# One decoder layer on one core: the last down group taken out of the block scheme, its free slots used for the mask tables, and three smaller moves

## The chip, the core and the metric

The kernel runs on one core of a Trainium2 chip. The metric is the device time of one execution in microseconds (us), lower is better. The engines that matter are TensorE (PE in the profile: matmuls, with PEld its weight loads), VectorE (DVE), ScalarE (ACT), GpSimd (POOL) and SyncE (SP, which here only issues loads and stores). Each engine runs its own list of instructions in the order in which the program wrote them. It stops at an instruction whose operand is not ready, and then everything behind that instruction on the same engine stops too.

## The reference, cut to what matters

256 tokens of width 2048 go through one layer: a gated feed-forward block (5632 hidden columns), a token mixer with three kinds of attention, and a second feed-forward block.

```python
def _swiglu(h, w_gu, w_down):
    gate, up = jnp.split(h @ w_gu, 2, axis=-1)
    return (jax.nn.silu(gate) * up) @ w_down

def reference(x, ...):
    x = x + 0.5 * _swiglu(_rmsnorm(x, ffn1_norm), ffn1_w_gu, ffn1_w_down)
    x = x + _token_mixing(_rmsnorm(x, mix_norm), ...)
    x = x + 0.5 * _swiglu(_rmsnorm(x, ffn2_norm), ffn2_w_gu, ffn2_w_down)
    return x
...
# mixer C, per head: three softmaxes, over 16 compressed blocks, over selected blocks, over a window
    o = gate[..., 0:1] * o_cmp + gate[..., 1:2] * o_slc + gate[..., 2:3] * o_win
...
    merged = (gates[:, :, 0] * (o_a @ w_branch_a) + gates[:, :, 1] * (o_b @ w_branch_b)
              + gates[:, :, 2] * (o_c @ w_branch_c))
    return merged @ w_out
```

## The kernel before

**Three products for one.** Every large matrix product is made of three passes in a rounded 32-bit format: an operand is split into a rounded part `hi` (ACT copies it) and the rest `lo` (DVE subtracts), and `products` (lines 158 to 160) does hi by hi, lo by hi and hi by lo. The activations are split once, when they are made. The weights are split as they arrive: `emit_split` (lines 116 and 117) makes one ACT copy and one DVE subtraction for each weight tile of 128 x 1024.

**Steps.** All weight work is a list of steps, `subs`. A step is one split weight tile and the matmuls that use it. A plain step has twelve matmuls of 512 columns (two row tiles of weights, two halves of the tokens, three products). There are six raw tiles for arriving weights and four pairs of split tiles; the split of a step is written some three steps ahead of its matmuls (`stream`). Side work, such as transposes, evacuations or attention, is written as Python generators, `chains`. A chain is spawned into a phase of the step ("pre": before the step's last split is written, "mid": after it, "pe": after its matmuls) with a gap in steps. So a gap decides where in each engine's list the next piece of side work stands. Nothing is reordered later.

**Feed-forward.** The 11 blocks of 512 hidden columns are worked in four groups, (0,3), (3,6), (6,9), (9,11). In a group, each block's gate and up products are made, `to_mid` transposes and splits the result into the tile `mid`, and then the group's part of the down product is added to `x_sb`. All products but the first block's are made in pairs of 512 output columns by `add_pair`: part of the contraction goes through a scheme of seven block products in place of eight, a step of six matmuls each. The scheme costs DVE more: sums of weight blocks (line 356, and two accumulating DMAs issued by POOL at lines 402 and 406), differences between PSUM banks (lines 395 and 398), and sums of the activations. Those are made by `sums`, from x by `combos_x` and, once a group, from the middle by `combos_m` (pieces at lines 288 to 292 and 204/205, `ffn_samX`, `ffn_samS`). Each pair takes up to six PSUM banks; `more_banks` and `fewer_banks` move two of the eight banks between the pair scheme (`mains`) and the side work (`banks`).

**Handing over.** `down_evac` (line 479) adds a finished bank pair to `x_sb`. After the last group it spawns `x_prep` of the next stage, which transposes x (line 234) and splits it into `xT` (lines 207 and 208).

**Tables.** The mixers need mask and distance tables. `build` starts at step 52 (`TABLES_AT`), and `build_tables` (lines 534 to 574) makes them in pieces four steps apart, with the `ffn_f` tiles of the first feed-forward block as scratch.

**Mixer C.** `unit_c` works one head on one block of 128 queries, 24 units in all. `apply_p` transposes the probabilities in blocks of 128 keys (line 914), ACT copies them from PSUM (line 921), and `pv` multiplies them with the values (line 1055). The compressed keys are one more block, of 32 rows: it has its own transposes, its own DVE copy (line 923) and its own product over 32 rows (line 1052).

**Merge.** `branch_evac` multiplies each branch's product with its gate (DVE) and adds it up on POOL (line 1154). After the third branch, `to_mT` transposes the sum (line 1133), spawned with a gap of one step.

Of the kernel before, what the change touches and what calls it, by code (L numbers as in the profile page):

```python
# [24 lines left out]
TABLES_AT = 52  # L25
# [22 lines left out]
def hybrid_trunk_kernel(ctx, tc, x, ffn1_norm, ffn1_w_gu, ffn1_w_down, mix_norm, w_in, qk_gain, sinks, cmp_pos,  # L48
# [202 lines left out]
    def add_ffn(norm, w_gu, w_down, done):  # L251
# [46 lines left out]

        def combos_x():
# [10 lines left out]
            yield from sums(*tmp, st["sax"])  # L310
# [133 lines left out]
        def to_mid(kt0):  # L444
# [19 lines left out]
            if kt0 == 0:  # L464
                spawn(combos_m(), "mid", 3)

        def up_evac(kt0, gap):
            def f(bank):
# [3 lines left out]
                spawn(to_mid(kt0), "pe", gap)  # L472
# [13 lines left out]
        for gi, (a, b) in enumerate(groups):  # L486
            for c in range(a, b):
                kt0 = 4 * (c - a)
                up = up_evac(kt0, 1 if c == 10 else 3)
# [8 lines left out]
        li, raw, n, width, mm, before, after, post = subs[-1]  # L498

        def end():  # L500
            after()
            fewer_banks()
        subs[-1] = (li, raw, n, width, mm, before, end, post)


    tabs, scratch = {}, []
# [23 lines left out]
    def build_tables():  # L530
# [12 lines left out]
        yield "mid", 4  # L543
        DVE.scalar_tensor_tensor(m1, D, 127.5, m0, op0=OP.is_le, op1=OP.mult)
        table(tabs["B"], D, m1, m2)
        yield "mid", 4
        DVE.scalar_tensor_tensor(m1, D, 128.5, m0, op0=OP.is_le, op1=OP.mult)
        table(tabs["A"][:, 0], D, m1, m2)
        for g, dil in ((1, 4), (2, 16)):
            yield "mid", 4  # L550
# [6 lines left out]
        yield "mid", 4  # L557
# [34 lines left out]
    def add_mix(done):  # L592
# [6 lines left out]
        def open_mix():  # L599
# [7 lines left out]
            st["vcmp"] = p.tile([32, 64], F32, name="vcmp")  # L607
# [21 lines left out]
            POOL.memset(st["Xs"].bitcast(F32)[:, :, 64:66], 0.0)  # L629

# [205 lines left out]
        def cmp_tail(i, bank):  # L836
# [25 lines left out]
            if i == 1:  # L862
                DVE.tensor_copy(st["vcmp"], b[:32, :64])
# [41 lines left out]
        def apply_p(sb, blocks, pv):  # L905
# [7 lines left out]
            for i, (c0, n) in enumerate(blocks):  # L913
                PE.transpose(place[i][:n], sb[:, c0:c0 + n], ident)
# [3 lines left out]
            full = sum(n == 128 for _, n in blocks)  # L918
            for src, i0, n in ((b, 0, min(full, 4)), (O[:, 256:], 4, full - 4)):
# [18 lines left out]
        def unit_a(h, qb):  # L938
# [21 lines left out]
            blocks = [(g * nk + 128 * kb, 128) for g in range(3) for kb in range(qb + 1)]  # L960
# [16 lines left out]
        def unit_b(pr, qb):  # L977
# [25 lines left out]
            blocks = [(i * nk + 128 * kb, 128) for i in range(2) for kb in range(qb + 1)]  # L1003
# [15 lines left out]
        def unit_c(h, qb):  # L1019
# [27 lines left out]
            blocks = [(32 + 128 * i, 128) for i in range(2 * qb + 2)] + [(0, 32)]  # L1047

            def pv(pt, i):
                c0, n = blocks[i]  # L1050
                if n == 32:
                    PE.matmul(O[:, 0:64], pt[:32, i], st["vcmp"], start=True, stop=True)
                    return
# [89 lines left out]
        def branch_evac(b, oc):  # L1143
            def f(bank):
# [11 lines left out]
                if b == 2:  # L1156
                    spawn(to_mT(mg, oc), "pe", 1)
# [118 lines left out]
    if "mix" in stages:  # L1276
        def build():
# [4 lines left out]
            yield "mid", 1  # L1282
# [29 lines left out]
```

## Time and profile before

| what | value |
|---|---|
| time, median of 3 runs | 2180.73 us (2180.51 to 2181.09) |
| time of the profiled execution | 2181.03 us |
| its span, first to last instruction | 2179.3 us |
| PE busy | 2144.9 us, 98% of the span |
| DVE busy | 1615.8 us, 74% |
| ACT busy | 1247.9 us, 57% |
| POOL busy | 145.5 us, 7% |
| matmul instructions | 10081 |

A row of a timeline has a start, a busy time, the engine, the line, the operation and its tiles, and in brackets the idle time ahead of it with what ended it. Matmuls overlap: a 512-column matmul is shown as 0.39 us long, but the next one starts 0.23 us after it. So PE's pace is read from start to start, not from the busy time.

### The profile page before, as it was taken

Reading aid. Unit: us, or ns where it says so; the run is one execution under the profiler, and the core shown is the slowest. Engines: PE = TensorE matmul, PEld = TensorE weight load, DVE = VectorE, ACT = ScalarE, POOL = GpSimd, SP = SyncE. Lnnn points to the kernel's source line nnn. Section 1 sums busy time; section 2 is a strip of 40 time slices with the busy share of each in tenths; the row PEclk is TensorE's granted clock in tenths of the full one; section 3 lists DMA queues with packets and bytes.
Section 4 is the critical chain, followed back from the end, with each engine's and each line's share of the span. In section 5 each row is a group of like instructions: output and inputs, shape, how many; then the busy total and the mean of one; then the engine's idle time right before and its main releaser. Section 6 shows DMA issues by size and latency. Waiting matters only on the chain. (4 is left out here: it accounts for less than half of the span.)

```text
span 2179.3 us, 27509 instructions
## 1 busy us (share of the span) xinstructions
PE 2144.9 (98%) x10081; PEld 1796.9 (82%) x10081; DVE 1615.8 (74%) x2050; ACT 1247.9 (57%) x1664; POOL 145.5 (7%) x155
## 2 busy tenths in 40 slices
PE   8999999999999999999999999999999999999998
PEld 6887888888887999998888788888888888888886
DVE  7988887888887676666555554557978887887886
ACT  6655665565565566555555444445655665665564
POOL 0000000000000121000000110100000000000000
PEclk9999999999999999999999999999999999999999
DMA  8887878888886574444456666567878878887974
GB/s 287 245 243 222 268 234 230 275 231 244 232 264 171 165 230 134 120 112 141 126 152 191 180 184 193 174 194 240 248 225 269 262 203 268 236 266 205 289 217 142
DMA packets 237600, 463.66 MB, mean 213 GB/s; under 512 B 13384, under 2 KB 42648, under 8 KB 234904
## 3 DMA queue, kind: packets, MB, share of 16 engines
q1 hardware_dynamic: 217368, 403.17, 56.0%
q0 software_dynamic: 20096, 58.72, 15.4%
q8 instruction: 79, 1.29, 0.2%
q14 instruction: 57, 0.47, 0.1%
HBM read 430.39 MB, written 2.10 MB: 198 GB/s over the span
## 5 line engine op out<-in xcount | busy, mean ns | idle before, releaser
L117 DVE TENSOR_TENSOR lo<-raw,hi 128x1024 fp32r<-128x1024 f32 (+3 forms) x561 | 663.9, 1186 | 310.6 <-ACT hi L116 299.1
L116 ACT ACTIVATE hi<-raw 128x1024 fp32r<-128x1024 f32 (+3 forms) x561 | 570.5, 1020 | 322.8 <-PE main L160 255.7
L116 ACT ACTIVATE hi<-ffn_sb 128x1024 fp32r<-128x1024 f32 x392 | 412.5, 1059 | 294.5 <-PE main L160 122.6
L158 PE MATMUL main<-hi,xT 128*128 128x512 f32 (+2 forms) x1480 | 567.7, 384 | 2.9 <-ACT hi L116 2.9
L117 DVE TENSOR_TENSOR lo<-ffn_sb,hi 128x1024 fp32r<-128x1024 f32 x392 | 473.1, 1222 | 125.6 <-ACT hi L116 121.3
L159 PE MATMUL main<-lo,xT 128*128 128x512 f32 (+2 forms) x1480 | 557.9, 377 | 3.2 <-DVE lo L117 3.2
L160 PE MATMUL main<-hi,xT 128*128 128x512 f32 (+2 forms) x1480 | 557.6, 377 | 0.0
L158 PEld LDWEIGHTS main<-hi,xT 128*128 128x128 f32 x1480 | 279.1, 189 | 55.0 <-issue 6.6
L159 PEld LDWEIGHTS main<-lo,xT 128*128 128x128 f32 x1480 | 278.7, 188 | 48.2 <-DVE lo L117 6.5
L160 PEld LDWEIGHTS main<-hi,xT 128*128 128x128 f32 x1480 | 278.3, 188 | 43.5
L159 PE MATMUL main<-lo,ffn_midt 128*128 128x512 f32 x348 | 136.0, 391 | 2.9 <-DVE lo L117 2.9
L158 PE MATMUL main<-hi,ffn_midt 128*128 128x512 f32 x348 | 136.3, 392 | 1.6 <-DVE main L398 1.4
L160 PE MATMUL main<-hi,ffn_midt 128*128 128x512 f32 x348 | 135.6, 390 | 0.0
L356 DVE TENSOR_TENSOR ffn_sb<-ffn_sb,ffn_sb 128x2048 f32<-128x2048 f32 (+1 forms) x72 | 130.9, 1818 | 2.5
L159 PE MATMUL misc<-lo,xT 128*128 128x512 f32 x296 | 115.5, 390 | 1.1 <-DVE lo L117 1.1
L160 PE MATMUL misc<-hi,xT 128*128 128x512 f32 x296 | 115.3, 389 | 0.0
L158 PE MATMUL misc<-hi,xT 128*128 128x512 f32 x296 | 115.3, 389 | 0.0
L159 PEld LDWEIGHTS main<-lo,ffn_midt 128*128 128x128 f32 x348 | 65.4, 188 | 17.7 <-DVE lo L117 4.5
L158 PEld LDWEIGHTS main<-hi,ffn_midt 128*128 128x128 f32 x348 | 65.4, 188 | 15.8 <-DVE main L398 1.8
L158 PE MATMUL misc<-hi,ffn_midt 128*128 128x512 f32 x196 | 76.7, 391 | 1.1 <-DVE misc L398 1.1
L160 PEld LDWEIGHTS main<-hi,ffn_midt 128*128 128x128 f32 x348 | 65.4, 188 | 13.5
L159 PE MATMUL misc<-lo,ffn_midt 128*128 128x512 f32 x196 | 76.4, 390 | 0.0
(276 smaller groups left out, 2742.0 us busy)
## 6 DMA issues: line engine op xcount, KB each, us to landing
raw<-in_ffn_w_gu_dram SPq DMA_DIRECT2D x192, 512.0 KB, 7.3
ffn_sb<-in_ffn_w_gu_dram SPq DMA_DIRECT2D x80, 1024.0 KB, 6.9
raw<-in_ffn_w_down_dram SPq DMA_DIRECT2D x112, 512.0 KB, 5.6
raw<-in_w_in_dram SPq DMA_DIRECT2D x96, 512.0 KB, 3.6
raw<-in_w_in_dram SPq DMA_DIRECT2D x88, 384.0 KB, 3.3
ffn_sb<-in_ffn_w_down_dram SPq DMA_DIRECT2D x64, 512.0 KB, 6.4
ffn_sb<-in_ffn_w_gu_dram POOLq DMA_DIRECT2D x20, 1024.0 KB, 9.8
ffn_sb<-ffn_sb POOLq DMA_DIRECT2D x20, 1024.0 KB, 8.1
```

Of the source, the lines that this page charges most:

```text
L116: ACT.activation(hi, raw, AF.Copy)
L117: DVE.tensor_tensor(lo, raw, hi.bitcast(F32), op=OP.subtract)
L158: PE.matmul(o, lhs(0), hi, start=start, stop=False, **kw)
L159: PE.matmul(o, lhs(0), lo, start=False, stop=False, **kw)
L160: PE.matmul(o, lhs(1), hi, start=False, stop=stop, **kw)
L356: DVE.tensor_tensor(block_buf(i, dst), block_buf(i, a), block_buf(i, b), op=OP.add)
```

## The change

Five edits, all in the order or the form of work:

1. **Last group plain.** For the group (9,11) the four output blocks of the down product are made by `add_chunk`, twelve matmuls a step, and no sums of the middle are made for it. The two banks go back to the side work ahead of that group (`late`), where `fewer_banks` stood at the stage's end.
2. **Tables.** `build` starts at step 90, and `build_tables` waits for `ready_late`, which the last group's first step sets. Its pieces are two steps apart where they were four.
3. **Sums of the middle** in eight pieces, four steps apart, where there were four pieces three steps apart.
4. **Merge transposes** spawned with a gap of two steps.
5. **Compressed values** padded with zero rows from 32 to 128, so that the compressed block is treated as the others are.

```diff
-TABLES_AT = 52
+TABLES_AT = 90
...
-        def sums(a11, a12, a21, a22, dst, gap=1):
-
-            DVE.tensor_tensor(a22, a21, a22, op=OP.subtract)
-            DVE.tensor_tensor(a21, a11, a21, op=OP.subtract)
-            yield "mid", gap
-            DVE.tensor_tensor(a11, a22, a11, op=OP.subtract)
-            DVE.tensor_tensor(a12, a12, a11, op=OP.add)
-            yield "mid", gap
+        def sums(a11, a12, a21, a22, dst, one, two):
+
+            for i, (d, a, b, op) in enumerate(((a22, a21, a22, OP.subtract), (a21, a11, a21, OP.subtract),
+                                               (a11, a22, a11, OP.subtract), (a12, a12, a11, OP.add))):
+                DVE.tensor_tensor(d, a, b, op=op)
+                if (two, one)[i % 2]:
+                    yield "mid", (two, one)[i % 2]
             for i, (n, t) in enumerate((("X5", a22), ("S2", a11), ("X3", a12), ("S3", a21))):
                 split_to(dst[n][:, :, 0], dst[n][:, :, 1], t)
-                if i == 1:
-                    yield "mid", gap
+                if (two, one)[i % 2] and i < 3:
+                    yield "mid", (two, one)[i % 2]
...
-            yield from sums(f[0][:, :, :128], f[1][:, :, :128], f[0][:, :, 128:], f[1][:, :, 128:], st["sam"], 3)
+            yield from sums(f[0][:, :, :128], f[1][:, :, :128], f[0][:, :, 128:], f[1][:, :, 128:], st["sam"], 4, 4)
...
+        def late():
+            fewer_banks()
+            ready_late.append(norm)
...
-            if kt0 == 0:
-                spawn(combos_m(), "mid", 3)
+            if blocks:
+                spawn(combos_m(), "mid", 2)
...
-            for j in (0, 2):
-                add_pair(w_down, 512 * a, 4 * (b - a), NSM, 512 * (j + 1), 512 * j, part_of("mid", st), "sam",
-                         down_evac(j + 1, gi == 3), down_evac(j, gi == 3))
+            for j in range(4):
+                evac = down_evac(j, gi == 3)
+                if b - a == 2:
+                    add_chunk(w_down, 512 * a, 4 * (b - a), 512 * j, 512, part_of("mid", st), evac,
+                              before=late if j == 0 else None)
+                elif j % 2:
+                    add_pair(w_down, 512 * a, 4 * (b - a), NSM, 512 * j, 512 * (j - 1), part_of("mid", st), "sam",
+                             evac, down_evac(j - 1, False))
...
-            st["vcmp"] = p.tile([32, 64], F32, name="vcmp")
+            st["vcmp"] = p.tile([128, 64], F32, name="vcmp")
...
+            POOL.memset(st["vcmp"], 0.0)
...
-            for i, (c0, n) in enumerate(blocks):
-                PE.transpose(place[i][:n], sb[:, c0:c0 + n], ident)
+            for i, c0 in enumerate(blocks):
+                PE.transpose(place[i], sb[:, c0:c0 + 128], ident)
...
-            if full < nb:
-                DVE.tensor_copy(pt[:32, full], place[full][:32])
...
-                    PE.matmul(O[:, 0:64], pt[:32, i], st["vcmp"], start=True, stop=True)
+                    PE.matmul(O[:, 0:64], pt[:, i], st["vcmp"], start=True, stop=True)
...
-                    spawn(to_mT(mg, oc), "pe", 1)
+                    spawn(to_mT(mg, oc), "pe", 2)
...
-            yield "mid", 1
+            while not ready_late:
+                yield "mid", 1
             yield from build_tables()
```

Two places show what moves. The first is DVE's list in the first group of the first feed-forward block, at the pair of the group's third hidden block; `raw` and `ffn_sb` are weight tiles, `lo` is what the split leaves. Before:

```order
L117 TENSOR_TENSOR lo_86<-ffn_sb_158,hi_82 128x1024
L356 TENSOR_TENSOR ffn_sb_158<-ffn_sb_158,ffn_sb_160 128x2048
L205 TENSOR_TENSOR ffn_samX_154<-ffn_f_165,ffn_samX_154 128x2x128
L205 TENSOR_TENSOR ffn_samS_155<-ffn_f_164,ffn_samS_155 128x2x128
L117 TENSOR_TENSOR lo_83<-raw_77,hi_79 128x1024
L117 TENSOR_TENSOR lo_84<-ffn_sb_158,hi_80 128x1024
```

After:

```order
L117 TENSOR_TENSOR lo_86<-ffn_sb_158,hi_82 128x1024
L355 TENSOR_TENSOR ffn_sb_158<-ffn_sb_158,ffn_sb_160 128x2048
L117 TENSOR_TENSOR lo_83<-raw_77,hi_79 128x1024
L290 TENSOR_TENSOR ffn_f_164<-ffn_f_165,ffn_f_164 128x2x128
L117 TENSOR_TENSOR lo_84<-ffn_sb_158,hi_80 128x1024
```

The two pieces between the 2048-wide block sum and the split of `raw_77` are gone from there; one shorter piece stands behind that split.

The second is DVE's list in the last down group of the first feed-forward block, where x gets its sums (line 479 before, 482 after) and `xT` is made (line 208). Before, in the pair scheme:

```order
L117 TENSOR_TENSOR lo_83<-ffn_sb_158,hi_79 128x1024
L356 TENSOR_TENSOR ffn_sb_158<-ffn_sb_158,ffn_sb_160 128x1024
L117 TENSOR_TENSOR lo_84<-raw_75,hi_80 128x1024
L117 TENSOR_TENSOR lo_85<-ffn_sb_158,hi_81 128x1024
L479 SCALAR_TENSOR_TENSOR x_sb<-main_64,x_sb 128x512
L479 SCALAR_TENSOR_TENSOR x_sb<-misc_70,x_sb 128x512
```

After, plain, with a piece of the tables (lines 553 to 557 and 540 to 542 there, 551 to 555 and 538 to 540 before):

```order
L117 TENSOR_TENSOR lo_83<-raw_77,hi_79 128x1024
L482 SCALAR_TENSOR_TENSOR x_sb<-main_65,x_sb 128x512
L482 SCALAR_TENSOR_TENSOR x_sb<-main_66,x_sb 128x512
L117 TENSOR_TENSOR lo_84<-raw_78,hi_80 128x1024
L553 TENSOR_SCALAR ffn_f_165<-ffn_f_164 128x256
L554 CAST ffn_f_165<-ffn_f_165 128x256
L555 CAST ffn_f_165<-ffn_f_165 128x256
L556 SCALAR_TENSOR_TENSOR ffn_f_165<-ffn_f_165,ffn_f_164 128x256
L557 TENSOR_TENSOR ffn_f_165<-ffn_f_165,ffn_f_164 128x256
L540 SCALAR_TENSOR_TENSOR tabA<-ffn_f_164,ffn_f_165 128x256
L541 TENSOR_SCALAR ffn_f_165<-ffn_f_165 128x256
L542 TENSOR_TENSOR tabA<-tabA,ffn_f_165 128x256
```

The block sums of line 356 are gone from the group, the sums into x stand behind a plain split, and eight table operations stand between two splits.

## Rows read from the trace of the kernel before

**Rows 1.** The page: busy times with instruction counts, PE's granted clock by slices.

```profile
PE 2144.9 (98%) x10081; PEld 1796.9 (82%) x10081; DVE 1615.8 (74%) x2050; ACT 1247.9 (57%) x1664; POOL 145.5 (7%) x155
...
PEclk9999999999999999999999999999999999999999
```

**Rows 2.** Waits of PE: line and releaser, us in total, times, longest.

```profile
PE main L159 <- DVE lo L117: 6.2, 10, 0.8
PE main L158 <- DVE x_sb L479: 5.7, 2, 2.9
PE misc L1133 <- POOL mg L1154: 4.5, 4, 1.1
...
PE main L158 <- DVE main L398: 1.4, 1, 1.4
...
PE misc L158 <- DVE misc L398: 1.1, 1, 1.1
...
PE main L158 <- DVE misc L395: 0.6, 1, 0.6
```

**Rows 3.** Stretches: length, PE, PEld, DVE, ACT, POOL busy (count), clock, DMA, GB/s.

```profile
664.10:724.90 60.80, 55.04 (x243) 43.56 (x242) 46.11 (x57) 35.09 (x54) 3.13 (x4) 0.97 0.61 160
2119.98:2175.39 55.41, 50.24 (x219) 39.63 (x217) 40.27 (x44) 26.11 (x31) 3.00 (x3) 1.00 0.54 147
...
695.30:698.00 2.70, 2.70 (x8) 2.09 (x9) 1.57 (x2) 0.06 (x1) 0.83 (x1) 0.56 0.93 245
...
2155.00:2175.00 20.00, 20.00 (x90) 16.54 (x89) 12.79 (x15) 7.43 (x7) 0.00 (x0) 1.00 0.23 69
```

**Rows 4.** Timeline, last down group of the first feed-forward block, PE.

```profile
695.29 0.48 PE L158 MATMUL main<-hi,ffn_samX 128*128 128x512 f32 x1 [2.84 <-DVE x_sb L479]
```

**Rows 5.** The handover to the mixer, DVE's groups of 695 to 733 us.

```profile
L208 DVE SCALAR_TENSOR_TENSOR xT<-misc,cols,xT 128x256 fp32r<-128x256 f32 x16 | 7.4, 481 | 7.5 <-ACT xT L207 7.5
```

**Rows 6.** Timeline, a piece of the tables on DVE, and PE behind it.

```profile
179.73 0.28 DVE L551 TENSOR_SCALAR ffn_f<-ffn_f 128x256 f32<-128x256 f32 x1
...
182.63 0.69 DVE L395 TENSOR_TENSOR misc<-ffn_s,main 128x512 f32<-128x512 f32 x1
...
183.47 0.47 PE L158 MATMUL main<-hi,ffn_samS 128*128 128x512 f32 x1 [0.57 <-DVE misc L395]
```

**Rows 7.** Timeline, sums of the middle on DVE in the second group, and PE.

```profile
292.68 0.42 DVE L205 TENSOR_TENSOR ffn_samX<-ffn_f,ffn_samX 128x256 fp32r<-128x256 f32 x1
...
293.35 1.22 DVE L117 TENSOR_TENSOR lo<-raw,hi 128x1024 fp32r<-128x1024 f32 x1
...
293.68 0.39 PE L158 MATMUL main<-hi,xT 128*128 128x512 f32 x1
294.63 0.50 PE L159 MATMUL main<-lo,xT 128*128 128x512 f32 x1 [0.56 <-DVE lo L117]
```

**Rows 8.** Timeline, the first merge: POOL's sums, then PE's transposes.

```profile
1196.90 3.50 POOL L1154 TENSOR_TENSOR mg<-mg,gate 128x512 f32<-128x512 f32 x2 [3.70 <-DVE gate L1153]
...
1199.05 0.27 PE L1133 MATMUL misc<-ident,mg 128*128 128x128 f32 x1
1200.46 0.55 PE L1133 MATMUL misc<-ident,mg 128*128 128x128 f32 x3 [1.13 <-POOL mg L1154]
```

**Rows 9.** PE's products with the values: a unit of mixer C, one of mixer A.

```profile
849.49 0.55 PE L1055 MATMUL misc<-VC,pt 128*128 128x64 f32 x4
849.98 0.43 PE L1052 MATMUL misc<-vcmp,pt 32*128 32x64 f32 x2
850.34 0.44 PE L158 MATMUL main<-hi,xT 128*128 128x384 f32 x1
...
1069.54 1.45 PE L965 MATMUL misc<-VA,pt 128*128 128x64 f32 x12
1070.82 0.28 PE L897 MATMUL misc<-ident,ob 128*128 128x128 f32 x1
```

**Rows 10.** The page: GB/s that the DMA engines moved, in 40 slices.

```profile
GB/s 287 245 243 222 268 234 230 275 231 244 232 264 171 165 230 134 120 112 141 126 152 191 180 184 193 174 194 240 248 225 269 262 203 268 236 266 205 289 217 142
```

More of the change, by code (lines that the diff above doesn't have):

```diff
@@ L309, in combos_x @@
                     yield "mid", 1
-            yield from sums(*tmp, st["sax"])
+            yield from sums(*tmp, st["sax"], 1, 0)
             load_block(0, "22", "21")
@@ L442, in gate_evac, with to_mid @@
                 DVE.scalar_tensor_tensor(m, bank[tb], r, m, op0=OP.mult, op1=OP.mult)
-        def to_mid(kt0):
+        def to_mid(kt0, blocks):
             m = st["m"]
@@ L460, in to_mid, with up_evac @@
                 split_to(st["mid"][:, k0:k0 + 2, 0], st["mid"][:, k0:k0 + 2, 1], b.rearrange("p (k t) -> p k t", k=2))
-                if kt0 == 0:
+                if blocks:
                     ACT.activation(st["f"][half], b, AF.Copy)
                 banks.give(b)
-            if kt0 == 0:
-                spawn(combos_m(), "mid", 3)
-        def up_evac(kt0, gap):
+            if blocks:
+                spawn(combos_m(), "mid", 2)
+        def up_evac(kt0, gap, blocks):
             def f(bank):
@@ L471, in f @@
                     DVE.scalar_tensor_tensor(m, bank[tb], rstd[norm][:, tb:tb + 1], m, op0=OP.mult, op1=OP.mult)
-                spawn(to_mid(kt0), "pe", gap)
+                spawn(to_mid(kt0, blocks), "pe", gap)
             return f
@@ L488, in add_ffn @@
                 kt0 = 4 * (c - a)
-                up = up_evac(kt0, 1 if c == 10 else 3)
+                up = up_evac(kt0, 1 if c == 10 else 3, c == a and b - a > 2)
                 if c == 0:
@@ L494, in add_ffn @@
                     add_pair(w_gu, 0, KT, NS, FF + 512 * c, 512 * c, part(xT), "sax", up, gate_evac)
-            for j in (0, 2):
-                add_pair(w_down, 512 * a, 4 * (b - a), NSM, 512 * (j + 1), 512 * j, part_of("mid", st), "sam",
-                         down_evac(j + 1, gi == 3), down_evac(j, gi == 3))
[L498 to L506, printed above, removed]
+            for j in range(4):
[6 more added lines that the diff above has]
+                             evac, down_evac(j - 1, False))
+    tabs, scratch, ready_late = {}, [], []
     def late_rows_in():
@@ L542, in build_tables @@
         table(tabs["C"], D, m0, m2)
-        yield "mid", 4
+        yield "mid", 2
         DVE.scalar_tensor_tensor(m1, D, 127.5, m0, op0=OP.is_le, op1=OP.mult)
         table(tabs["B"], D, m1, m2)
-        yield "mid", 4
+        yield "mid", 2
         DVE.scalar_tensor_tensor(m1, D, 128.5, m0, op0=OP.is_le, op1=OP.mult)
@@ L549, in build_tables @@
         for g, dil in ((1, 4), (2, 16)):
-            yield "mid", 4
+            yield "mid", 2
             DVE.tensor_scalar(m1, D, 1.0 / dil, None, op0=OP.mult)
@@ L556, in build_tables @@
             table(tabs["A"][:, g], D, m1, m2)
-        yield "mid", 4
+        yield "mid", 2
         dc = D[:, :64].rearrange("p (q n) -> p q n", q=2)
@@ L862, in cmp_tail @@
             if i == 1:
-                DVE.tensor_copy(st["vcmp"], b[:32, :64])
+                DVE.tensor_copy(st["vcmp"][:32], b[:32, :64])
                 banks.give(b)
@@ L917, in apply_p @@
             pt = st["pt"].take()
-            full = sum(n == 128 for _, n in blocks)
-            for src, i0, n in ((b, 0, min(full, 4)), (O[:, 256:], 4, full - 4)):
+            for src, i0, n in ((b, 0, min(nb, 4)), (O[:, 256:], 4, nb - 4)):
                 if n > 0:
                     ACT.activation(pt[:, i0:i0 + n], src[:, :128 * n].rearrange("p (k q) -> p k q", q=128), AF.Copy)
-            if full < nb:
-                DVE.tensor_copy(pt[:32, full], place[full][:32])
             banks.give(b)
@@ L959, in unit_a @@
             yield "pe", 1
-            blocks = [(g * nk + 128 * kb, 128) for g in range(3) for kb in range(qb + 1)]
+            blocks = [g * nk + 128 * kb for g in range(3) for kb in range(qb + 1)]
             def pv(pt, k):
@@ L1002, in unit_b @@
             yield "pe", 1
-            blocks = [(i * nk + 128 * kb, 128) for i in range(2) for kb in range(qb + 1)]
+            blocks = [i * nk + 128 * kb for i in range(2) for kb in range(qb + 1)]
             def pv(pt, k):
@@ L1046, in unit_c @@
             yield "pe", 1
-            blocks = [(32 + 128 * i, 128) for i in range(2 * qb + 2)] + [(0, 32)]
+            blocks = [32 + 128 * i for i in range(2 * qb + 2)] + [0]
             def pv(pt, i):
-                c0, n = blocks[i]
-                if n == 32:
-                    PE.matmul(O[:, 0:64], pt[:32, i], st["vcmp"], start=True, stop=True)
+                c0 = blocks[i]
+                if c0 == 0:
+                    PE.matmul(O[:, 0:64], pt[:, i], st["vcmp"], start=True, stop=True)
                     return
```

## The prediction

> **What bounds the kernel now.** I read the busy times first. PE is busy 98% of the span at the full granted clock (2.4 GHz) and every other engine far less [rows 1], so the time is PE's list plus the holes in it. An edit counts only by matmul time that it adds or takes, and by holes that it closes or opens. Then I read PE's waits [rows 2]. They are few and have places: DVE being late with `lo` (10 waits), with the sum into x (2) and with PSUM differences (lines 395 and 398, three waits); and POOL being late with the merged sum (4). Last I read single holes on the timeline, and took for each what stood ahead of the late instruction on the late engine.
>
> Two prices recur. A plain stretch without a hole holds 88 starts of 512-column matmuls in 20.00 us [rows 3] (90 are counted, two had begun before it), so one costs 0.227 us. And a hole costs more than its idle time, because PE also overlaps less around it: where 0.56 us of idle is shown, starts are 294.63 - 293.68 = 0.95 us apart in place of 0.227, so 0.72 us are lost [rows 7].
>
> **The change part by part.**
>
> *Last group plain.* The pair scheme spends per pair 7 block products of 6 matmuls and 4 plain steps of 12, 90 in all; plain it is 96. Two pairs in each of two feed-forward blocks make 24 more matmuls, 24 x 0.227 = 5.4 us added, all on PE's path. Against that stand the holes of this group. In the first block, the stretch from the last three gate/up steps to the first step of the mixer takes 60.80 us with 242 starts, 210 of 512 columns and 32 transposes (one more had begun before it) [rows 3]. At 0.227 and 0.109 us (the transposes' distance in the trace, as the three that follow the wait in the merge show within 0.02 us [rows 8]) they need 47.7 + 3.5 = 51.2 us, so 9.6 us are lost there. The largest piece is one hole of 2.84 us, where a product needs a bank that the sum into x still reads, and that sum stands on DVE behind two splits [rows 4]. PE's granted clock is 0.56 in the stretch behind it [rows 3], so most of that runs at the 1.2 GHz level. Plain, a chunk takes only two of four banks and the sum has a whole chunk of four steps to finish; nobody waits for a 2048- or 1024-wide block sum, since none is made; and PSUM differences fall away. The later work on `mid` has time as well: the last block's transposes stand behind a step of 12 matmuls, where 6 stood, and its split is due two steps later.
>
> What is late next is DVE, since the tables now lie here. Its work in the group by rows: 16 splits of 1.22 [rows 7], four sums into x of 1.2 to 1.4, three `xT` blocks of (7.4 + 7.5) / 4 = 3.7 with their idle time [rows 5], and tables. A dilated piece takes 182.63 - 179.73 = 2.9 us [rows 6]; two of them, three shorter ones at half of it and a small last one are some 11.5 us. Together 47 us against PE's 16 x 2.72 + 3.5 = 47.1 us. So DVE just keeps up. But around the second dilated piece it is late: by the list, the third sum into x then comes about a step late, and its transposes wait. I leave 1.5 us of holes in the first block and 0.4 in the second, where no tables are. First block: 222 x 0.227 + 3.5 + 1.5 = 55.4, 5.4 us less than 60.8. Second block: 55.41 us with 210 + 8 starts now [rows 3], 222 x 0.227 + 0.9 + 0.4 = 51.7 after, 3.7 us less.
>
> *Tables out of the first group.* The waits on lines 395 and 398 (0.6 + 1.4 + 1.1 = 3.1 us idle [rows 2]) all fall in the first group of the first block, each behind a piece of the tables as in [rows 6]; the other groups have the same PSUM differences and no such wait. By 0.72 / 0.56 they come to 4.0 us; one small hole of that kind stays in any group, so they are worth 3.9 us. The small loads and the one transpose of `build` move from step 52 to 90; on SP's queue they stand ahead of one raw load and on DVE they add a copy behind a sum that waits for PE anyway. I cost them at nothing; if that cover is gone, it is the copy's 0.2 us.
>
> *Sums of the middle in eight pieces.* Of the ten waits for `lo`, six are like [rows 7]: two pieces (293.35 - 292.68 = 0.67 us) stand between a 2048-wide block sum and a split that PE already waits for. One for each of three groups in two blocks. PE's starts are 0.95 us apart there, 0.72 lost. Without the pieces the split ends 0.67 us earlier. That is 4.0 us by the pieces alone and 5.0 if the slow start behind the hole goes as well; I take 4.3. The pieces come back singly, 0.34 us each, between splits where DVE now waits for ACT's `hi`, so I cost them at nothing; if one meets a late split, it is 0.3 us for each of six groups.
>
> *Merge a step later.* Four times the second transpose waits for POOL: starts 1.41 us apart in place of 0.11, so 1.3 us are lost [rows 8]. POOL's two sums take 3.5 us; a further step of twelve matmuls (2.7 us) lies in between now and covers the 1.13 us that were short. 4 x 1.3 = 5.1 us. The bank and the `mg` tile come free a step later; two tiles and four free banks allow that.
>
> *Compressed values padded.* In mixer C, four products and the compressed one (two instructions) take 850.34 - 849.49 = 0.85 us; in mixer A twelve instructions over 128 rows take 1.28 us, 0.107 each [rows 9]. Six at 0.107 are 0.64 us, so a unit saves 0.21, and there are 12 heads x 2 query blocks = 24 units: 5.0 us, up to 0.24 x 24 = 5.8 if the last one overlaps with what follows as it does in mixer A. I take 5.3. ACT copies 12 blocks more on their own and 12 within a larger copy; ACT is busy 57% [rows 1] and nothing waits for it there. DVE loses 24 copies.
>
> The Trainium skill (TensorE: Matmul & The Clock Gate, Why this matters for your kernels) says of one product over 32 rows that it takes the time of one over 128. By that this edit would give nothing, a rival below. The Trainium skill (TensorEngine Tiling (Array Packing), Key Properties) says that changing the tiling mode drains the engine, which fits the 0.85 us.
>
> *Sum.* -5.4 - 3.7 - 3.9 - 4.3 - 5.1 - 5.3 = -27.7 us on the profiled 2181.03 us (its span of 2179.3 and 1.7 around it): 2153.3. The median lies 0.3 lower, so **2153.0 us**, 1.3% faster.
>
> **The rivals.**
>
> (a) *DVE sets the pace of the last group.* The tables cost there what they cost in the first group, 3.9 us, on top of the 1.5. For it: 47 against 47.1 us. Against it: four split tiles let DVE be three steps late before PE feels it. 2157 us.
>
> (b) *Padding gives nothing*, since a 32-row product costs a 128-row one and the 0.2 us belong to something else, such as the change of bank or of the weights' source. Against it: the products over 128 rows in the same unit change the weights' source as often and are not slow. 2158.3 us.
>
> (c) *The holes only move.* PE runs ahead of DVE by what was gained and meets it at the next block sum, so that the sums' 4.3 and half of the group's 9.1 come back: 2162 us. Against it: DVE waits for ACT right behind those places, thus has slack.
>
> (d) *Slower: the weights of the last group arrive too slowly.* Plain, all of them go through the six raw tiles, 0.52 MB per 2.72 us, 193 GB/s; before, half came early into the block tiles. At the slowest slice's 112 GB/s [rows 10] a step would take 4.7 us, 2.0 us more in 32 steps: 2153 + 63 = 2216 us. It decides from 141 GB/s down (3.7 us a step, which eats 32 us). Against it: six tiles are 16 us of lead, and the mixer's slices with 512-wide plain steps move 180 to 194 GB/s [rows 10] while PE waits for no weights [rows 2]. The low slices are low by demand.
>
> **How the numbers follow.** A difference under 0.2% (4.4 us) can hardly be told from none. My forecast, 2150 to 2155.5, gets 0.68; (a) 0.10; (b) 0.08; (c) 0.07; (d) 0.03; a small mishap that eats the gain to within 0.2%, 0.04. The forecast's lower end takes the sums at 5.0, the padding at 5.8 and no holes in the last group (-3.1): 2149.9, rounded down to 2149. The upper end takes in (a) and (b): 2160. Faster 0.93, same 0.04, slower 0.03.
>
> **What would show it.** Right: PE's matmul count up by 24 and no 32-row rows; no wait of PE for x_sb of 2.8 us, for lines 395/398 or for POOL's merge; the stretch of the first block's last group near 55.4 us; compressed products in the same 0.107 us as their neighbours; at most six small waits for `lo`, under 0.2 us each. Wrong: PE waiting for `lo`, `mid` or x_sb in the last group for more than 3 us in all, or any wait for raw weights there.

## The result, and the profile after

The changed kernel takes 2151.51 us (median of 4 runs, 2150.21 to 2151.93) against 2180.68 us for the kernel before: a ratio of 0.9865, 95% interval 0.9848 to 0.9882, so 29.2 us or 1.3% faster. 2153.0 was predicted, with 2149 to 2160 as the range. The profiled execution has a span of 2149.9 us, 29.4 less than the one before. Since PE is busy almost throughout, the comparison goes by PE: I took the starts of the same matmuls in both traces and compared the legs between them.

| leg, from one landmark of PE to the next | before us | after us | difference | forecast |
|---|---|---|---|---|
| start to the first 512-column matmul | 9.34 | 9.71 | +0.37 | none |
| to the last three gate/up steps of the first block | 654.76 | 646.91 | -7.84 | tables -3.9, half of the sums -2.15 |
| its last group, to the first step of the mixer | 60.81 | 57.17 | -3.65 | -5.4 |
| to mixer C's first product with the compressed keys | 103.37 | 102.55 | -0.81 | none |
| mixer C, to its last compressed product with the values | 183.32 | 178.03 | -5.28 | -5.3 |
| to the last product with the merged sum, `mT` (four legs) | 463.04 | 457.51 | -5.53 | -5.1 |
| to the last three gate/up steps of the second block | 645.34 | 641.40 | -3.94 | half of the sums -2.15 |
| its last group, to the last matmul | 55.03 | 52.35 | -2.68 | -3.7 |
| to the end | 4.27 | 4.27 | 0.00 | none |

One thing is needed to read the table. Of the last group's 180 matmuls with `mid`, six stood ahead of the last three gate/up steps in the kernel before, and all 192 stand behind that point now. Six matmuls, 1.36 us, have moved from the longer legs into the last groups' legs. Like for like the last groups gained 3.65 + 1.36 = 5.0 and 2.68 + 1.36 = 4.0 us, and the two legs ahead of them 7.84 - 1.36 = 6.5 and 3.94 - 1.36 = 2.6. Without the start, the legs sum to -29.7 us, where -27.7 was forecast.

The page's busy times, after:

```profile
span 2149.9 us, 27410 instructions
PE 2135.9 (99%) x10105; PEld 1798.6 (84%) x10105; DVE 1571.9 (73%) x1982; ACT 1231.6 (57%) x1644; POOL 138.2 (6%) x148
```

PE has the 24 matmuls more that were counted (10105 against 10081 in [rows 1]). The waits of PE after (line and releaser, us in total, times, longest), as in [rows 2]:

```profile
PE main L158 <- ACT hi L116: 3.2, 1, 3.2
PE misc L520 <- DMA rows<-in_ffn_norm_dram: 2.5, 1, 2.5
PE misc L234 <- DMA x_sb<-in_x_dram: 1.5, 2, 1.4
PE misc L234 <- DVE x_sb L482: 1.1, 2, 0.8
PE main L159 <- DVE lo L117: 1.0, 2, 0.8
PE misc L917 <- DVE oT L205: 0.4, 2, 0.2
PE misc L884 <- DVE kc L879: 0.2, 1, 0.2
```

The first three rows are the start of the program. Of the rest, the wait of 5.7 us for x_sb, POOL's 4.5 us for the merge and the three waits for PSUM differences are gone. The two waits for `lo` that are left lie at 53.9 and 59.8 us, in the first pair of the program, where they stood before. Only one place in the rest of the program has a hole of over 0.2 us: a hand-over in the first block's last group, 1.1 us.

The last groups as stretches (length, PE, PEld, DVE, ACT, POOL busy with counts, clock, DMA share, GB/s), as in the first two of [rows 3]:

```profile
656.60:713.77 57.17, 55.97 (x261) 46.01 (x260) 44.91 (x79) 28.89 (x45) 1.29 (x25) 1.00 0.54 163
2093.27:2145.63 52.36, 52.36 (x236) 43.43 (x235) 26.91 (x28) 17.97 (x18) 0.00 (x0) 1.00 0.44 146
```

In the second block PE has no hole at all, and the clock is full in both. DVE, with the tables, is busy 44.91 of 57.17 us in the first block. What this does to PE is on the timeline of the third hand-over, first PE's transposes of the new x, then DVE's list ahead of them:

```profile
704.18 0.33 PE L234 MATMUL misc<-ident,x_sb 128*128 128x128 f32 x1 [0.79 <-DVE x_sb L482]
704.78 0.44 PE L234 MATMUL misc<-ident,x_sb 128*128 128x128 f32 x2 [0.27 <-DVE x_sb L482]
```

```profile
692.49 0.29 DVE L553 TENSOR_SCALAR ffn_f<-ffn_f 128x256 f32<-128x256 f32 x1
...
695.39 0.48 DVE L208 SCALAR_TENSOR_TENSOR xT<-misc,cols,xT 128x256 fp32r<-128x256 f32 x1
...
698.78 2.36 DVE L117 TENSOR_TENSOR lo<-raw,hi 128x1024 fp32r<-128x1024 f32 x2 [0.46 <-ACT hi L116]
701.06 0.19 DVE L564 TENSOR_SCALAR ffn_f<-ffn_f 128x64 f32<-128x64 f32 x1
...
702.30 1.22 DVE L117 TENSOR_TENSOR lo<-raw,hi 128x1024 fp32r<-128x1024 f32 x1
703.44 1.28 DVE L482 SCALAR_TENSOR_TENSOR x_sb<-main,x_sb 128x512 f32<-128x512 f32 x2
```

The second dilated piece of the tables takes DVE from 692.49 to 695.39, ahead of the `xT` block, and the small last piece from 701.06 to 702.30, ahead of the split behind which the sum into x stands. PE's last matmul of the chunk began at 703.00; then it waited for that sum.

The other two edits in rows: the first merge, POOL's sum and PE's transposes (four at once, no wait, where [rows 8] has 1.13 us), and a unit of mixer C with the padded product (0.20 us for the pair of instructions, where [rows 9] has 0.36):

```profile
1180.80 2.29 POOL L1155 TENSOR_TENSOR mg<-mg,gate 128x512 f32<-128x512 f32 x1
```

```profile
1184.43 0.60 PE L1134 MATMUL misc<-ident,mg 128*128 128x128 f32 x4
```

```profile
837.30 0.55 PE L1056 MATMUL misc<-VC,pt 128*128 128x64 f32 x4
837.68 0.39 PE L1053 MATMUL misc<-vcmp,pt 128*128 128x64 f32 x2
837.88 0.42 PE L158 MATMUL main<-hi,xT 128*128 128x384 f32 x1
```

### The profile page after: what moved, and what is told of

Same layout as the page of the kernel before. It is cut to its first block, busy times and chain, and to the rows that moved or that the text cites. A ratio compares the mean times of both kernels' runs of the same rounds, so it can differ in the third digit from the quotient of the medians.

```text
span 2149.9 us, 27410 instructions
## 1 busy us (share of the span) xinstructions
PE 2135.9 (99%) x10105; PEld 1798.6 (84%) x10105; DVE 1571.9 (73%) x1982; ACT 1231.6 (57%) x1644; POOL 138.2 (6%) x148
## 4 chain that ended last, share of the span: by engine, by line
PE 96%; DVE 2%; issue 1%; ACT 1%; DMA 0%; POOL 0%; SPq 0%; ACTq 0%; DVEq 0%; POOLq 0%
PE main L158 24%; PE main L159 23%; PE main L160 23%; PE misc L160 6%; PE misc L158 6%; PE misc L159 6%; PE misc L459 1%; PE misc L917 1%; DVE lo L117 1%; PE misc L1056 1%; PE misc L1027 1%; DMA raw<-in_ffn_w_gu_dram 0%; PE misc L946 0%; ACT hi L116 0%; PE misc L1028 0%
## 5 line engine op out<-in xcount | busy, mean ns | idle before, releaser
L117 DVE TENSOR_TENSOR lo<-raw,hi 128x1024 fp32r<-128x1024 f32 (+3 forms) x577 | 681.9, 1186 | 352.0 <-ACT hi L116 341.8
L116 ACT ACTIVATE hi<-raw 128x1024 fp32r<-128x1024 f32 (+3 forms) x577 | 588.1, 1023 | 359.2 <-PE main L160 290.5
L116 ACT ACTIVATE hi<-ffn_sb 128x1024 fp32r<-128x1024 f32 x364 | 383.4, 1060 | 264.7 <-PE main L160 113.8
L117 DVE TENSOR_TENSOR lo<-ffn_sb,hi 128x1024 fp32r<-128x1024 f32 x364 | 438.4, 1222 | 116.0 <-ACT hi L116 112.2
L158 PE MATMUL main<-hi,ffn_midt 128*128 128x512 f32 x420 | 164.3, 391 | 0.0
L160 PE MATMUL main<-hi,ffn_midt 128*128 128x512 f32 x420 | 163.5, 389 | 0.0
L159 PE MATMUL main<-lo,ffn_midt 128*128 128x512 f32 x420 | 163.4, 389 | 0.0
L160 PEld LDWEIGHTS main<-hi,ffn_midt 128*128 128x128 f32 x420 | 78.8, 188 | 16.5
L158 PEld LDWEIGHTS main<-hi,ffn_midt 128*128 128x128 f32 x420 | 78.8, 188 | 16.2
L159 PEld LDWEIGHTS main<-lo,ffn_midt 128*128 128x128 f32 x420 | 78.9, 188 | 16.0
L159 PEld LDWEIGHTS misc<-lo,xT 128*128 128x128 f32 x296 | 55.6, 188 | 11.6
L160 PEld LDWEIGHTS misc<-hi,xT 128*128 128x128 f32 x296 | 55.6, 188 | 11.6
```

The costliest lines, as they stand in the source:

```text
L116: ACT.activation(hi, raw, AF.Copy)
L117: DVE.tensor_tensor(lo, raw, hi.bitcast(F32), op=OP.subtract)
L158: PE.matmul(o, lhs(0), hi, start=start, stop=False, **kw)
L159: PE.matmul(o, lhs(0), lo, start=False, stop=False, **kw)
L160: PE.matmul(o, lhs(1), hi, start=False, stop=stop, **kw)
```

## The experiments

The theory was the prediction's: six terms that add up, each with its place. The rivals that could still be right after such a result were that terms make up for each other, that the padding works by something other than the count of rows, that the sums gain by their number and not by their place, and that the tables in the last group cost as much as they save. Each run starts from the kernel before (e1 to e6) or from the changed one (e7 to e11). "The leg" below is the one of the table above. Single spans differ by the start: over the profiles here the first 512-column matmul begins between 7.2 and 10.0 us. The leg behind the start differs too, by up to 0.9 us (e2: +0.89, with nothing changed there), all of it in the first 60 us. From there on, legs that an edit leaves alone agree to 0.1 us, but for one place in e6. Only the last groups' legs in e1 to e5 differ more, by up to 2.4 us, for the most part by the clock (last section).

### Padding alone, to 128 and to 64 rows

```diff
-            st["vcmp"] = p.tile([32, 64], F32, name="vcmp")
+            st["vcmp"] = p.tile([128, 64], F32, name="vcmp")     # e2: [64, 64]
...
-            blocks = [(32 + 128 * i, 128) for i in range(2 * qb + 2)] + [(0, 32)]
+            blocks = [(32 + 128 * i, 128) for i in range(2 * qb + 2)] + [(0, 128)]     # e2: (0, 64)
...
-                    PE.matmul(O[:, 0:64], pt[:32, i], st["vcmp"], start=True, stop=True)
+                    PE.matmul(O[:, 0:64], pt[:, i], st["vcmp"], start=True, stop=True)      # e2: pt[:64, i]
```

> The kernel before with the padding alone, the DVE copy of the compressed block now over 128 rows. Theory (each change between 32 and 128 contraction rows makes PE run empty): the 24 compressed products go from 0.85 us with their four neighbours to 0.64, 5.0 to 5.8 us less, 2175.4. Rival (a 32-row product costs a 128-row one, the gain of the full change lies elsewhere): 2180.7, no change.

> The same with 64 rows. If it is the change of row count that costs, 64 rows cost what 32 did and nothing is gained: 2180.7 (at most 0.5 us off). If a product is dear because it has few rows, about a third to a half of the padding's gain shows: 2178 to 2179.

In both, `vcmp` is set to zero first. In e2 DVE still copies the compressed block, over 64 rows. In e1 there is no DVE copy any more, unlike what the expectation says: ACT copies the block with the others, as in the changed kernel.

Measured: with 128 rows 2176.82 against 2181.33 us, ratio 0.9978 (0.9969 to 0.9988), and mixer C's leg -5.28 us, to the hundredth what the changed kernel shows. With 64 rows 2181.58 us, ratio 0.9998 (0.9989 to 1.0008), and that leg +0.03. PE's timeline of e2, a unit of mixer C:

```profile
848.21 0.55 PE L1056 MATMUL misc<-VC,pt 128*128 128x64 f32 x4
848.69 0.43 PE L1053 MATMUL misc<-vcmp,pt 64*128 64x64 f32 x2
849.05 0.44 PE L158 MATMUL main<-hi,xT 128*128 128x384 f32 x1
```

From the four products to the next step it is 0.84 us with 64 rows, 0.85 with 32 [rows 9] and 0.58 with 128. So the price doesn't fall with more rows: what costs is that two instructions of another row count stand among those of 128. The DVE copy is not the cause: in the kernel before, the one for the unit of [rows 9] ends at 847.1 us, and the product starts at 849.98. The kernel before also has longer runs of products over 64 rows, in mixer A:

```profile
1007.45 0.93 PE L946 MATMUL misc<-KA,QA 64*128 64x128 f32 x6
1008.31 0.44 PE L158 MATMUL main<-hi,xT 128*128 128x384 f32 x1
```

In the trace the next start is 0.21 us behind the first of the six, 0.11 behind each of the four that follow, and 0.20 behind the last. Transposes of the same width over 128 rows are 0.11 us apart. So 64 rows run at the pace of 128 as long as the row count stays, and each change costs some 0.10 us.

Rival (b) is out, and with it the change of bank or of the weights' source as the cause. The measured price is 5.28 / 24 = 0.22 us for one unit, going there and back. The Trainium skill (TensorEngine Tiling (Array Packing), Key Properties) says that a change of the tiling mode drains the engine. e2 agrees in so far as the change costs and the number of rows doesn't; no row here shows whether it is a drain.

### Merge transposes a step later, alone

```diff
-                    spawn(to_mT(mg, oc), "pe", 1)
+                    spawn(to_mT(mg, oc), "pe", 2)
```

> The kernel before with the merge's transposes a step later and nothing else. Theory: four waits of 1.1 us idle (1.3 from start to start) go, 5.1 to 5.5 us less: 2175.4. Rival (the later transposes push the splits of the merged tile into the output product, which then waits for them): 2179 to 2181.

Measured: 2176.16 against 2181.33 us, ratio 0.9979 (0.997 to 0.9988). The three legs of the merge change by +2.72, -6.77 and -1.34 us (the first only because the first transpose comes a step later), -5.39 in all, each to the hundredth as in the changed kernel. The four waits for POOL are gone. The term is independent of the rest. The 0.13 us more that the changed kernel gains over its four legs come with the padding: they are in e1 too.

### The block sums of the middle, by number and by place

e4 makes the eight single pieces of the change in the first three groups of each block and leaves the last group as it was. e5 keeps the four double pieces and lets the chain begin one step later.

```diff
-                spawn(combos_m(), "mid", 3)
+                spawn(combos_m(last), "mid", 3 if last else 2)   # e4, with eight yields in combos_m
```

```diff
-                spawn(combos_m(), "mid", 3)
+                spawn(combos_m(), "mid", 3 if last else 4)       # e5
```

> The kernel before with the sums of the middle in eight pieces four steps apart in the first three groups of both blocks; the last group's stay as they were. Theory: six waits of 0.56 us idle go, 4.0 to 5.2 us less: 2175.5 to 2176.7. Rival (DVE is simply short of time there and the same work waits elsewhere): 2179 to 2181, with new waits of PE for lo.

> The kernel before with the four double pieces of the sums kept and spawned one step later in the first three groups. If the place decides (the pieces stand between a 2048-wide block sum and a split that PE waits for), the six waits go here too: 2175.5 to 2176.7. If the number of pieces decides, two pieces in one place are late wherever they stand, and it stays at 2180 to 2181 or moves by waits of 0.5 us at other lines.

Measured: e4 2175.56 against 2181.33 us, ratio 0.9977 (0.9967 to 0.9986); e5 2176.82 against 2181.61, ratio 0.9979 (0.997 to 0.9988). The clean measure is the two legs ahead of the last groups, in which these sums are made: -2.52 and -2.67 in e4, 5.2 us; -2.06 and -1.94 in e5, 4.0 us. DVE's timeline in e4 and in e5, around the place of [rows 7]:

```profile
287.95 2.29 DVE L368 TENSOR_TENSOR ffn_sb<-ffn_sb,ffn_sb 128x2048 f32<-128x2048 f32 x1
290.16 1.22 DVE L117 TENSOR_TENSOR lo<-raw,hi 128x1024 fp32r<-128x1024 f32 x1
291.29 0.42 DVE L322 TENSOR_TENSOR ffn_f<-ffn_f,ffn_f 128x256 f32<-128x256 f32 x1
```

```profile
286.51 0.42 DVE L291 TENSOR_TENSOR ffn_f<-ffn_f,ffn_f 128x256 f32<-128x256 f32 x1
286.96 0.42 DVE L292 TENSOR_TENSOR ffn_f<-ffn_f,ffn_f 128x256 f32<-128x256 f32 x1
287.31 2.35 DVE L117 TENSOR_TENSOR lo<-ffn_sb,hi 128x1024 fp32r<-128x1024 f32 x2
289.69 2.29 DVE L356 TENSOR_TENSOR ffn_sb<-ffn_sb,ffn_sb 128x2048 f32<-128x2048 f32 x1
291.90 1.22 DVE L117 TENSOR_TENSOR lo<-raw,hi 128x1024 fp32r<-128x1024 f32 x1
```

In both no piece stands between the wide block sum and the split any more. PE's first matmul of that step begins at 291.61 in e4, with the `lo` one at 291.83, the regular 0.22 us behind. In e5 they are 0.28 us apart and the one after 0.34:

```profile
292.89 0.39 PE L158 MATMUL main<-hi,xT 128*128 128x512 f32 x1
293.18 0.50 PE L159 MATMUL main<-lo,xT 128*128 128x512 f32 x1
293.51 0.39 PE L160 MATMUL main<-hi,xT 128*128 128x512 f32 x1
```

So the place gives 4.0 of the 5.2 us: 0.67 for each of the six holes, exactly the two pieces taken out of DVE's list there. In e5 a double piece stands in the step ahead (286.51) instead, and DVE is still a few hundredths late: that leaves 0.06 + 0.11 us each time, 1.0 us over six places. With single pieces the split is early enough and the slow restart goes as well.

### The last group plain, alone

```diff
-                spawn(to_mid(kt0), "pe", gap)
+                spawn(to_mid(kt0, blocks), "pe", gap)
...
+                if b - a == 2:
+                    add_chunk(w_down, 512 * a, 4 * (b - a), 512 * j, 512, part_of("mid", st), evac,
+                              before=fewer_banks if j == 0 else None)
```

The tables stay in the first group.

> The kernel before with the last group plain in both blocks and all else as before, the tables at step 52. Theory: 24 matmuls more (5.4 us) against the holes of both last groups (9.6 and 6.7 us), and with no tables in the group none of the 1.5 us left open for it: 10.0 to 11.5 us less, 2169.2 to 2170.7. Rival (the tables are no load in the last group): 9.1 us less as in the full change, 2171.6.

Measured: 2170.48 against 2181.61 us, ratio 0.9948 (0.9934 to 0.9963). The last groups' legs: -5.49 and -2.68. The stretch of the first block's last group in e6:

```profile
663.80:719.12 55.32, 55.32 (x263) 46.19 (x262) 34.73 (x44) 28.95 (x46) 0.00 (x0) 1.00 0.54 169
```

PE has no hole in it: 55.32 us is the plain group's own length. (228 matmuls at 0.227 us and 3.5 us of transposes are 55.3.) The leg to mixer C's first key product is 0.85 us shorter here as in the changed kernel, so that gain, which the prediction did not have, belongs to this edit: behind the pair scheme DVE was still behind at the fourth hand-over, where PE waited for x_sb at 727.8 us; it no longer does. In the leg ahead of the second block's last group 0.9 us of the expected 1.36 is missing: two late `lo` at 1843 and 1849 us, which no other run has.

### The tables back in the first group

```diff
-TABLES_AT = 90
+TABLES_AT = 52
...
-            while not ready_late:
-                yield "mid", 1
+            yield "mid", 1
```

The pieces are four steps apart, as in the kernel before; all else is the changed kernel.

> The changed kernel with the tables put back to step 52, four steps apart. Theory: the three waits at the PSUM differences of the first group return (3.9 us), and the two waits of PE for x_sb in the last group (1.4 and 0.3 us from start to start) go: 2.2 us more than the changed kernel, 2153.7. Rival (the sums in eight pieces, not the tables, freed DVE in the first group): no return of those waits, 2149.8.

Measured: 2152.66 us (2152.31 to 2153.07), ratio 0.9869 (0.9852 to 0.9885). Against the changed kernel's trace the leg ahead of the last group is 4.30 us longer and the last group 1.85 shorter (55.32 us, as in e6). Of the 4.30, 0.4 lies in the first 60 us of the program, where no tables are yet, so 3.9 belongs to the tables and the move is worth 3.9 - 1.85 = 2.1 us. Both ends are visible. In e7 these waits of PE are back:

```profile
PE main L158 <- DVE main L397: 1.4, 1, 1.4
...
PE misc L158 <- DVE misc L397: 1.1, 1, 1.1
...
PE main L158 <- DVE misc L394: 0.6, 1, 0.6
```

and the x_sb wait of the last group is gone. So the tables cost 1.85 us where they are now and 3.9 where they were. The medians show 1.2 us of it; in the profiles, e7's first 512-column matmul began 1.8 us earlier than the changed kernel's.

### The tables let go a step or two sooner, and thinned

```diff
+        def gate_last(bank):
+            gate_evac(bank)
+            ready_late.append(norm)
...
-                    add_pair(..., "sax", up, gate_evac)
+                    add_pair(..., "sax", up, gate_last if c == 10 else gate_evac)
```

(`ready_late` is no longer set in `late`.) e8 and e10 are this kernel. e9 is the changed kernel again, timed beside e10. e11 is e10 with four steps in place of two ahead of the small last piece.

> The changed kernel with the tables let go at the last gate product, some five steps ahead of the last down group, where DVE idles 0.9 to 1.5 us in each step. Theory: the wait of PE for x_sb at the third hand-over (0.79 us idle, 1.4 from start to start) and the small one before it go: 1.4 to 1.7 us less than the changed kernel, 2149.9. Rival (that wait belongs to the four xT pieces at the same place, not to tables): 2151.5, the same.

> The changed kernel once more, unaltered, as the yardstick for the two that follow. Expected 2151.5 us (2150.2 to 2152.5), 0.9865 of the kernel before. How much its first matmul varies (x's DMA and the first split) is to be seen as well: differences of 1 us between single profiles are no evidence unless the leg they lie in is named.

> The kernel of e8 once more, in one call with the changed kernel. In e8's profile the last group's stretch was 56.37 us against 57.17, so 0.8 us shorter; the 2.3 us at the start were x's DMA. Theory (DVE's list ahead of the sum into x is what makes the third hand-over late): 0.8 us below the changed kernel of the same call. Rival (all of e8's gain was the start): the same as the changed kernel within 0.3 us, with the gain of the last group lost in the gate/up steps before it, since the tables' first pieces now stand there.

> The kernel of e8, and the last small piece of the tables (the compressed branch's, with the sink and the gain, 1.25 us of DVE) let go two steps later, so that it stands behind the second sum into x instead of ahead of it. That sum came 0.36 us late in e8, and PE waited 0.27 us more for its second half. Theory: the sum comes 1.25 us sooner, no wait for x_sb in the last group is left, and the stretch is 55.4 us, 1.0 us below e8 and 1.8 below the changed kernel. Rival: the hole only moves to the third sum into x, behind which the piece now stands with its xT blocks; then the stretch stays at 56.4 us.

| run | median us (range) | ratio to before (95%) | last group's leg us |
|---|---|---|---|
| e8 | 2149.79 (2149.32 to 2150.11) | 0.9855 (0.984 to 0.9869) | 56.37 |
| e9, the changed kernel | 2151.17 (2150.05 to 2152.0) | 0.9865 (0.9851 to 0.988) | 57.17 |
| e10 | 2149.91 (2149.0 to 2150.61) | 0.9861 (0.9844 to 0.9877) | 56.39 |
| e11 | 2149.96 (2149.01 to 2150.79) | 0.986 (0.9845 to 0.9875) | 56.13 |

The 0.8 us of e8 in the last group come again in e10, so they are real; the rival that all of it was the start falls. Nor are they lost in the leg ahead: that is 0.8 us longer in e8 than in the changed kernel's first profile, but all of it in the first 60 us of the program, and in e10 it is 0.1 longer than in e9. It is half of what e8 was to give. The third hand-over has no hole any more, but the second has one now, since the dilated pieces stand a chunk earlier. PE in e10:

```profile
690.17 0.33 PE L234 MATMUL misc<-ident,x_sb 128*128 128x128 f32 x1 [0.39 <-DVE x_sb L485]
690.76 0.77 PE L234 MATMUL misc<-ident,x_sb 128*128 128x128 f32 x5 [0.27 <-DVE x_sb L485]
```

e11 was to take this one away and took a quarter of it: 56.13 us where 55.4 was expected, and no difference in the median. The small piece (1.25 us) was moved behind the sum, and the sum into x came only 0.3 us sooner. DVE in e11:

```profile
684.71 2.36 DVE L117 TENSOR_TENSOR lo<-raw,hi 128x1024 fp32r<-128x1024 f32 x2 [0.46 <-ACT hi L116]
687.97 1.23 DVE L117 TENSOR_TENSOR lo<-raw,hi 128x1024 fp32r<-128x1024 f32 x1 [0.90 <-ACT hi L116]
689.11 1.28 DVE L485 SCALAR_TENSOR_TENSOR x_sb<-main,x_sb 128x512 f32<-128x512 f32 x2
```

Where the piece had stood, DVE now idles 0.90 us for ACT's `hi`: the split ahead of the sum was not ready either. In e7 DVE idles the same 0.90 us there, but counted from the last three gate/up steps everything at this hand-over stands 2.4 us later in e11. ACT is late because it shares the `xT` copies with DVE. ACT at that hand-over, in e11 and in e7 (without tables there):

```profile
681.84 0.84 ACT L207 ACTIVATE xT<-misc,cols 128x256 fp32r<-128x256 f32 x2 [2.94 <-DVE xT L208]
```

```profile
683.48 0.84 ACT L207 ACTIVATE xT<-misc,cols 128x256 fp32r<-128x256 f32 x2 [0.55 <-DVE xT L208]
```

The dilated piece in front of DVE's first `xT` copy holds ACT up by 2.4 us (2.94 against 0.55), and ACT's next splits with it. So the expectation counted the DVE instructions ahead of the sum and left out the wait inside them. A version with the tables in the last group but none ahead of an `xT` block was not tried.

Whether e10 or e11 beats the changed kernel: the medians lie 1.2 to 1.3 us lower, 0.8 to 1.0 of it is seen in the one leg, the four runs of each overlap with those of e9 in 2150.05 to 2150.79. I take it as 0.8 us, too little for the whole-run ratios to tell (0.9861 and 0.9865, with intervals of 6 to 7 us).

## Why the prediction was right, point by point

The places and the mechanisms of the six terms were right, each shown by a run of its own. The legs give 2.0 us more than the sum: 0.9 by the sums of the middle, 0.8 by a hand-over that the sum didn't have, and 0.3 by the merge. Two of the signs that were named for a right prediction didn't come: the last group's stretch was to be near 55.4 us and is 57.17, and one wait for `lo` is longer than 0.2 us, the one of 0.8 in the program's first pair, which was there before.

**Padding, -5.3.** Measured -5.28, 0.22 us for a unit, where 0.21 to 0.24 was forecast. The cause named from the timeline (row count) is shown by e1 and e2.

**Merge, -5.1.** Measured -5.4 (e3, and the changed kernel in the same legs): each of the four holes was worth 1.35 us, a little more than the 1.3 read from one start to the next.

**Tables out of the first group, -3.9.** Measured: 7.84 - 1.36 for the six matmuls - 2.58 for the sums (3.94 - 1.36 in the second block) = 3.9. "They are worth 3.9 us" holds, and e7 gives it back (4.30, less the 0.4 at the program's start).

**Sums of the middle, -4.3 within 4.0 to 5.0.** Measured 5.2 (2.58 in each block): a little over the upper bound, where 4.3 was taken. The lower bound, "4.0 us by the pieces alone", is what e5 measures, and "5.0 if the slow start behind the hole goes as well" what e4 does. The choice between the two was wrong: nothing was left at the split, since DVE then came early enough for PE to feel no hole at all. A hole is worth 0.72 us to the next start and 0.86 with the two starts behind it. The count of six holes is right, but not "of the ten waits for `lo`": four are in that row of [rows 2], and two in the row for the bank `misc`, which stands there by itself:

```profile
PE misc L159 <- DVE lo L117: 1.1, 2, 0.6
```

**Last group plain, -5.4 and -3.7.** Measured like for like -5.0 and -4.0. The step that was mis-sized is the count: "222 x 0.227 + 3.5 + 1.5 = 55.4". It is 228, because six matmuls of the group lay ahead of the stretch before and lie in it now; so the stretch grew by 1.36 us and the one ahead of it shrank by as much, and only the sum of the two was right. The hole was well placed ("the third sum into x then comes about a step late, and its transposes wait": 704.18) and measured 1.85 us by e6 and e7, where 1.5 was left. In the second block no hole is left, where 0.4 was. Part of the first block's gain is chance: the 60.80 us that the forecast starts from hold a fall of the clock behind the hole, which other executions of the same group don't have there (58.93 us in e5, 59.39 in e1). What it comes to on average stands in the section on the hardware.

**Costed at nothing.** The weights (rival (d)): PE waits for none, 163 GB/s in the stretch. The moved small loads: no wait. Not seen in advance: the hand-over to the mixer, -0.8 us.

**The rivals.** (a) would have needed the tables to cost 3.9 + 1.5 in the last group; they cost 1.85. (b) falls with e1 and e2. (c) falls with e3, e4 and e6, whose gains add up to the whole: -5.3 - 5.4 - 5.2 - 10.8 (e6 without its start) - 2.1 (the tables' move) make -28.8, against -29.7 in the changed kernel's trace without its start; the 0.9 us that e6 lost at two splits is the difference. No gain came back elsewhere.

## What to carry to other kernels

When one engine is busy throughout, cost an edit by its starts: count the matmuls in the very stretch whose length is quoted, and check that both ends mean the same instruction in the new order. When side work has to go somewhere, look at what it stands ahead of and at who else waits for that: a piece in front of a copy that two engines share delays both, and taking one piece away gains only up to the next wait in the list. Give a lone product the row count of its neighbours.

## What the runs showed of the hardware

**The same hole sometimes lowers the clock and sometimes doesn't.** Before the change each block's last group has one hole of some 2.85 us. The stretch of 2.7 us right behind it has the clock at 0.56 in the first block [rows 3], but full in the second, in the same execution:

```profile
2150.65:2153.35 2.70, 2.70 (x12) 2.26 (x13) 1.58 (x2) 1.05 (x2) 0.82 (x1) 1.00 0.91 266
```

In e5, where these groups are as before, it is the other way round (first block, second block):

```profile
692.58:695.28 2.70, 2.70 (x16) 2.35 (x17) 1.63 (x3) 0.96 (x2) 0.81 (x1) 1.00 0.91 242
2145.24:2147.94 2.70, 2.70 (x7) 2.19 (x8) 1.58 (x2) 0.07 (x1) 0.82 (x1) 0.56 0.91 267
```

The legs follow: first block 60.81 us with the lower level behind the hole (before) and 58.93 without (e5); second block 55.03 without and 57.40 with it. In e1 they are 59.39 without and 56.95 with it. So a fall to the 1.2 GHz level costs 1.4 to 2.4 us here, on top of the hole. All six traces with this hole in both blocks have the fall behind one of the two: behind the first block's in the kernel before, e2, e3 and e4 (0.56, 0.65, 0.50 and 0.76 in the stretch of 2.7 us), behind the second's in e1 and e5 (0.52 and 0.56). The other block's stretch is at 1.00 each time.

The result of each run also lists the mean granted clock of every execution, and it goes with the time. Of the 51 executions of the kernel before that were timed beside the experiments, 8 have 1.000 and take 2179.2 us on average, 19 have 0.999 (2181.0 us), 21 have 0.998 (2182.3 us) and 3 have 0.997 (2183.8 us). All 28 executions of kernels with the plain last group (the changed one and e6 to e11) have 1.000. This accounts for much of the difference in spread: 7 us over the 51 (2178.2 to 2185.6), 2 over the 8 of the changed kernel (2150.0 to 2152.0). The 51 take 2181.4 us on average, 2.2 more than the 8 without a fall. So by an estimate from these means some 2 us of what the change gains are falls of the clock that no longer happen. They belong to the last group's terms; neither the prediction nor e6 takes them apart from the holes. Where the falls lie in an execution is seen only in the traced ones.

**A change of row count costs about 0.22 us there and back**, with 64 rows as with 32 (e1, e2), and runs of 64-row products cost nothing but the two changes (line 946).
